# Stores issued from a loop, and x spread over block diagonals by masked ANDs, in a batched x yT product

## The chip, the cores and the metric

The kernel runs on one core of a Trainium2 chip. The metric is the device time of one execution in microseconds (us), smaller being better. Before the change it is 301.15 us, the median of three runs between 301.08 and 301.67 us.

## The reference

```python
batch, n_heads, seq_t, seq_s, channels = 8, 12, 512, 512, 64
# x, y: float32 [8, 12, 512, 64]
np.einsum('bhtc,bhsc->bhts', x, y).astype(np.float32)
```

There are 96 independent heads. For each of them a 512 x 64 matrix x is multiplied by the transpose of a 512 x 64 matrix y, which gives 512 x 512 float32 numbers. The inputs are 25.17 MB together and the output is 100.66 MB.

## The kernel before, in words

**Groups and halves.** The 96 heads are cut into NG = 6 groups of 16 heads. One load brings the x or the y of a group: 128 partitions with 16 KB each, 2 MB in all. So there are 12 loads, numbered n = 0 to 11, in the order x, y, x, y. Each group is computed in two halves, so there are NH = 12 steps i, and each step yields V = 4 output tiles of 2 MB (128 partitions x 4096 float32). That makes 48 stores, numbered o = 4*i + h.

**Buffers.** Five slots of 2 MB (`slots`) serve the loads first and the stores afterwards; results go into the four slots named in HOMES = (0, 2, 4, 1). ScalarE, VectorE and GpSimd cast the loaded float32 data to bf16 (`compress`): x goes to a tile `xk`, y is written in pairs into 32-bit words (`yb`). Two tiles `xb`, one for each half, hold x spread out for the product: every 32-bit word has two bf16 places, and in each 32-partition block only one of them is filled and the other stays zero from a memset at the start. `mix(i, name, part)` writes one of four 32-partition blocks of that spread with a strided copy on the engine `name`. VectorE then turns `xb` into `xT` and `yb` into `yT` in 32 x 32 blocks of 32-bit words (`transposes`).

**Products and evictions.** TensorE runs a loop of 6 turns (`products`), two steps in a turn, 32 matmuls a step, into two PSUM tiles `pm`. ScalarE runs a loop of 11 turns (`evictions`), one step in a turn: for each of the four output tiles it waits until the earlier store out of that slot has landed (semaphore `out`), then copies two PSUM tiles of 128 x 2048 float32 into the slot. The first step's evictions stand ahead of the loop, among the casts.

**Order.** The order of the work on each engine is the order in which the program emits it; `emit` derives the waits, and with `virtual=True` it only keeps the books for instructions that a loop issues. Up to load 11 the casts of all loads, the spreads of steps 0 to 2 (by GpSimd) and the first four results are interleaved by hand. After that `prepare(i)` puts on VectorE the two transposes of step i and the four spreads of step i + 1. SyncE issues every DMA: the 12 loads (`load`) and the 48 stores, one after another, each behind a wait on the semaphore `taken`, which counts evictions.

Of the kernel before, what the change touches and what calls it, by code (L numbers as in the profile page):

```python
# [10 lines left out]
def kernel(  # L11
# [22 lines left out]
    nc = tc.nc  # L34
    B, H, T, C = x.shape
    _, _, S, _ = y.shape
    P = 128
    G = 16
    Q = P // G
    R = T // Q  # L40
    NG = B * H // G
    NH = 2 * NG
    V = G // 4
    K = 8
    E = R // K
    D = 32
    SLOTS = 5
    HOMES = (0, 2, 4, 1)
    fp32 = mybir.dt.float32
    bf16 = mybir.dt.bfloat16  # L50
    u32 = mybir.dt.uint32
    COPY = mybir.ActivationFunctionType.Copy
    assert C == 2 * D and S == T and R == 2 * D and Q * V == D
# [3 lines left out]
    ov = out.rearrange("b h t s -> (b h t s)").rearrange(  # L57
        "(o u h q n) -> o h q u n", u=2, h=V, q=Q * E, n=K * S
    )

    sb = ctx.enter_context(tc.tile_pool(name="sb", bufs=1))
    ps = ctx.enter_context(tc.tile_pool(name="ps", bufs=1, space=bass.MemoryType.PSUM))
    slots = [sb.tile([P, K * S], fp32, name=f"slot{i}") for i in range(SLOTS)]
    xks = [sb.tile([P, R, C], bf16, name=f"xk{i}") for i in range(NG - 1)]
    ybs = [[sb.tile([P, R // 2 * D], u32, name=f"yb{h}{i}") for i in range(NG - 1 + h)] for h in range(2)]
    xbs = [sb.tile([P, K * E * D], u32, name=f"xb{half}") for half in range(2)]
    xTs = [sb.tile([P, K * D * E], u32, name=f"xT{i}") for i in range(2)]
    yTs = [sb.tile([P, D * R // 2], u32, name=f"yT{i}") for i in range(2)]
    pms = [ps.tile([P, 4, S], fp32, name=f"pm{i}") for i in range(2)]
    engines = {"act": nc.scalar, "dve": nc.vector, "pool": nc.gpsimd, "pe": nc.tensor, "sp": nc.sync}  # L70
# [3 lines left out]
    def sem(p):  # L74
        if p not in sems:
            sems[p] = tc.alloc_semaphore(p)
        return sems[p]
# [19 lines left out]
    def emit(name, make, reads=(), writes=(), dma=None, tells=None, virtual=False):  # L97

        points = [writer[r] for r in (*reads, *writes) if r in writer]
        points += [v for w in writes for v in readers.get(w, ())]  # L100
        if name == "pool" and name in ticks:
            points.append((name, ticks[name]))
        need(name, points, virtual)
        p, step = (tells or name, 1) if dma is None else (dma, 16)
        sem(p)
        at = (p, ticks.get(p, 0) + step)
        ticks[p] = at[1]
        snaps[at] = {**known[name], p: at[1]}
        if dma is None:
            own[name][p] = at[1]  # L110
            snaps[at].update(own[name])
        if not virtual:
            make().then_inc(sems[p], step)
        for r in reads:
            readers.setdefault(r, []).append(at)
        for w in writes:
            writer[w], readers[w] = at, []

    made_slots, loaded, asked = [], {}, []
    in_front = ["dve", "pool", "dve", "act"]  # L120

    def copy(name, dst, src, reads, writes, tells=None, virtual=False):
        emit(
            name,
            lambda: nc.scalar.activation(dst, src, COPY)  # L125
            if name == "act"
            else engines[name].tensor_copy(dst, src),  # L127
            reads,
            writes,
            tells=tells,  # L130
            virtual=virtual,
        )

    def both(i):
        return [("slot", i, 0), ("slot", i, 1)]
# [14 lines left out]
    def compress(n):  # L150

        i = loaded.pop(n)
        g = n // 2
        if n % 2 == 0:
            xk = g % (NG - 1)
            dst = xks[xk].rearrange("p r c -> p (r c)")
            copy("act", dst, slots[i], both(i), [("xk", xk)])
            return
        ys = slots[i].rearrange("p (r c) -> p r c", c=C)
        for half in range(2):  # L160
            b = g % (NG - 1 + half)
            yv2 = ybs[half][b].bitcast(bf16).rearrange("p (j c w) -> p j w c", j=R // 2, w=2)
            for ch in range(2):
                copy(
                    in_front[2 * half + ch],
                    yv2[ch * 64:(ch + 1) * 64],
                    ys[half * 64:(half + 1) * 64, :, ch * D:(ch + 1) * D].rearrange(
                        "p (j w) c -> p j w c", w=2
                    ),
                    both(i),  # L170
                    [("yb", half, b, ch)],
                )

    def mix(i, name, part):

        g, half = divmod(i, 2)
        ch, u = divmod(part, 2)
        lo = half * 64 + u * D
        xk = g % (NG - 1)
        xv2 = xbs[half].bitcast(bf16).rearrange("p (k e c u) -> p k e c u", k=K, e=E, u=2)  # L180
        copy(
            name,
            xv2[part * D:(part + 1) * D, :, :, :, u],
            xks[xk][lo:lo + D, :, ch * D:(ch + 1) * D].rearrange("p (e k) c -> p k e c", k=K),
            [("xk", xk)],
            [("xb", half, part)],
        )

    def transposes(i):
        g, half = divmod(i, 2)  # L190
        b = g % (NG - 1 + half)
        emit(
            "dve",
            lambda: nc.vector.transpose(  # L194
                xTs[half].rearrange("p (k r e) -> p k e r", k=K, e=E),
                xbs[half].rearrange("p (k e c) -> p k e c", k=K, e=E),
            ),
            [("xb", half, part) for part in range(4)],
            [("xT", half)],
        )  # L200
        emit(
            "dve",
            lambda: nc.vector.transpose(  # L203
                yTs[half].rearrange("p (r j) -> p j r", r=D),
                ybs[half][b].rearrange("p (j c) -> p j c", c=D),
            ),
            [("yb", half, b, ch) for ch in range(2)],
            [("yT", half)],
            tells="turned",
        )  # L210

# [20 lines left out]
    def rows(s, pm):  # L232
        return slots[s].rearrange("p (r s) -> p r s", s=S)[:, 4 * pm:4 * pm + 4, :]

    def evictions():

        act = mybir.EngineType.Activation
        with nc.Fori(0, NH - 1, engines=OrderedEngineSet([act])) as turn:  # L238
            filled, free = turn + 2, turn * 16 + 16
            for h, s in enumerate(HOMES):  # L240
                nc.scalar.wait_ge(sem(f"out{s}"), free)
# [4 lines left out]
    def result(o):  # L246

        i, h = divmod(o, V)
        s = HOMES[h]
        for pm in range(2):  # L250
            emit("pe", None, [("xT", i % 2), ("yT", i % 2)], [("pm", pm)], tells=f"pe{h}{pm}", virtual=True)
            want = {"turned": i + 1, "taken": 2 * o + pm + 1}
            assert all(want.get(p, 0) >= v for p, v in asked[-1].items()), (o, pm, asked[-1])
            copy("act", rows(s, pm), pms[pm], [("pm", pm)], [("slot", s, pm)], "taken", virtual=i > 0)
            want = {f"pe{h}{pm}": i + 1, f"out{s}": 16 * i}
            assert i == 0 or all(want.get(p, 0) >= v for p, v in asked[-1].items()), (o, pm, asked[-1])
        emit("sp", lambda: nc.sync.dma_start(ov[i, h], slots[s]), reads=both(s), dma=f"out{s}")

    def prepare(i):

        if i < NH:
            transposes(i)
        if i + 1 < NH:
            for part in range(4):
                mix(i + 1, "dve", part)

    with tc.tile_critical():  # L267
        sem("taken")
        ticks["taken"] = 2
        for g in range(SLOTS):  # L270
            load(g)
        for half, name in enumerate(("dve", "pool")):
            emit(
                name,
                lambda: engines[name].memset(xbs[half], 0.0),  # L275
                writes=[("xb", half, part) for part in range(4)],
            )
        for n in range(2 * NG):
            if n == 11:
                result(3)  # L280
            compress(n)
            mix(n // 4, "pool", n % 4)
            if n == 4:
                transposes(0)
            if n < 5:
                load(n + SLOTS)
            elif n in (6, 8):
                load(n // 2 + 7)
            elif n < 10:
                assert slot() == HOMES[n // 2 - 2]  # L290
            if n > 7 and n < 11:
                result(n - 8)
            if n == 9:
                transposes(1)
        prepare(2)
        for o in range(V, V * NH):
            result(o)
            if o % V == V - 1:
                prepare(o // V + 2)
        products()  # L300
        evictions()
        for name, i in zip(("dve", "pool", "sp", "act"), HOMES):
            need(name, [(f"out{i}", ticks[f"out{i}"])])


# [28 lines left out]
```

## Time and profile before

| What | us |
|---|---|
| median of 3 runs | 301.15 (301.08 to 301.67) |
| profiled execution | 301.3 |
| its span in the profile | 299.5 |
| busy: ScalarE | 212.2 |
| busy: VectorE | 151.9 |
| busy: TensorE matmuls | 143.5 |
| busy: GpSimd | 56.1 |
| DMA queue, share of the 16 DMA engines' span | 98.8% |

The span is the time between the first and the last recorded instruction; the profiled execution took 1.8 us more than its span. Busy times of the engines overlap. The DMA share is the time that packets took, over 16 engines times the span. A landing is the moment at which the semaphore of a DMA has received all its increments.

### The profile page before, as it was taken

The numbers are of one execution on the slowest core, as the hardware profiler recorded it, in microseconds if no ns is written. First come the engines' busy times: TensorE is split into PE (matmuls) and PEld (weight loads), VectorE is DVE, ScalarE is ACT, GpSimd is POOL, SyncE is SP. The second block draws the span as 40 slices with busy tenths as digits, with TensorE's granted clock in tenths as the row PEclk, the third lists the DMA queues.
The fourth block names the chain that finished last, engine by engine and source line by source line (L and its number), as shares of the span: only waits on it lengthen the run. The fifth ranks groups of instructions, "written<-read, shape, count | busy, mean of one in ns | idle before, by whom it ended". The sixth has DMA issues, their size and how long they took to land.

```text
span 299.5 us, 1309 instructions
## 1 busy us (share of the span) xinstructions
PE 143.5 (48%) x378; PEld 36.8 (12%) x384; DVE 151.9 (51%) x73; ACT 212.2 (71%) x109; POOL 56.1 (19%) x23
## 2 busy tenths in 40 slices
PE   0000040556666555667556566647576568576100
PEld 0000010111111111111111111111111111111000
DVE  2157897999839490760934908629159070000000
ACT  1665576999999868686867777776768686868500
POOL 2399999991000000000000000000000000000000
PEclk9999999978799786775686775685776855776855
DMA  7999999999999999999999999999999999999995
GB/s 274 429 429 433 429 429 425 429 429 427 431 435 427 429 438 427 429 433 431 429 435 431 423 433 435 427 427 438 427 422 433 429 425 429 431 424 425 429 427 217
DMA packets 8641, 125.84 MB, mean 420 GB/s; under 512 B 960, under 2 KB 960, under 8 KB 960
## 3 DMA queue, kind: packets, MB, share of 16 engines
q1 hardware_dynamic: 8640, 125.83, 98.8%
q14 instruction: 1, 0.01, 0.0%
HBM read 25.17 MB, written 100.66 MB: 420 GB/s over the span
## 4 chain that ended last, share of the span: by engine, by line
DMA 66%; ACT 17%; issue 7%; DVE 2%; PE 1%; SPq 0%; ACTq 0%
DMA out_dram<-slot 52%; ACT slot L244 12%; DMA slot<-in_y_dram 7%; DMA slot<-in_x_dram 6%; ACT slot L125 3%; DVE yb L127 2%; ACT yb L125 1%; PE pm L226 1%; ACT xk L125 1%; SPq L145 0%; ACTq L238 0%; ACTq L243 0%; ACTq L92 0%; SPq L329 0%; SPq L267 0%
## 5 line engine op out<-in xcount | busy, mean ns | idle before, releaser
L226 PE MATMUL pm<-yT,xT 128*128 128x512 bf16 x378 | 143.5, 524 | 135.2 <-ACT slot L244 77.3
L244 ACT ACTIVATE slot<-pm 128x2048 f32<-128x2048 f32 x88 | 160.1, 1878 | 47.7 <-DMA out_dram<-slot 47.6
L194 DVE STREAM_TRANSPOSE xT<-xb 128x2048 uint32<-128x2048 uint32 x12 | 46.8, 3897 | 74.7 <-PE pm L226 72.3
L226 PEld LDWEIGHTS pm<-yT,xT 128*128 128x128 bf16 x384 | 36.8, 117 | 241.3 <-ACT slot L244 137.4
L127 DVE COPY xb<-xk 32x2048 bf16<-32x2048 bf16 x36 | 46.9, 1303 | 1.0
L127 DVE CAST yb<-slot 64x2048 bf16<-64x2048 f32 x12 | 36.2, 3017 | 16.9 <-DMA slot<-in_y_dram 16.7
L127 POOL COPY xb<-xk 32x2048 bf16<-32x2048 bf16 x12 | 36.3, 3023 | 10.4 <-ACT xk L125 9.6
L125 ACT ACTIVATE xk<-slot 128x4096 bf16<-128x4096 f32 x6 | 21.7, 3617 | 16.3 <-DMA slot<-in_x_dram 16.3
L203 DVE STREAM_TRANSPOSE yT<-yb 128x1024 uint32<-128x1024 uint32 x12 | 23.1, 1923 | 0.0
L125 ACT ACTIVATE yb<-slot 64x2048 bf16<-64x2048 f32 x6 | 14.8, 2462 | 5.1 <-DMA slot<-in_y_dram 5.1
L127 POOL CAST yb<-slot 64x2048 bf16<-64x2048 f32 x6 | 17.8, 2970 | 1.3 <-DMA slot<-in_y_dram 0.8
L125 ACT ACTIVATE slot<-pm 128x2048 f32<-128x2048 f32 x8 | 14.5, 1869 | 0.2 <-PE pm L226 0.2
L275 DVE MEMSET xb<- 128x2048 uint32 x1 | 1.8, 1765 | 1.4 <-SPq L267 1.4
L125 ACT ACT_TABLE_LOAD x1 | 1.3, 1283 | 0.9 <-SPq L267 0.9
L275 POOL MEMSET xb<- 128x2048 uint32 x1 | 1.8, 1805 | 0.5 <-SPq L267 0.5
L318 POOL MEMSET const-float32-0.0<- 128x1 f32 x1 | 0.1, 98 | 0.2 <-issue 0.2
L318 POOL MEMSET const-float32-1.0<- 128x1 f32 x1 | 0.1, 98 | 0.0
L318 POOL MEMSET const-bfloat16-1.0<- 128x1 bf16 x1 | 0.1, 98 | 0.0
L318 POOL MEMSET const-uint8-127<- 128x1 uint8 x1 | 0.1, 98 | 0.0
## 6 DMA issues: line engine op xcount, KB each, us to landing
out_dram<-slot SPq DMA_DIRECT2D x48, 2048.0 KB, 16.0
slot<-in_x_dram SPq DMA_DIRECT2D x6, 2048.0 KB, 17.6
slot<-in_y_dram SPq DMA_DIRECT2D x6, 2048.0 KB, 20.8
```

Of the source, the lines that this page charges most:

```text
L125: lambda: nc.scalar.activation(dst, src, COPY)
L127: else engines[name].tensor_copy(dst, src),
L194: lambda: nc.vector.transpose(xTs[half].rearrange("p (k r e) -> p k e r", k=K, e=E), xbs[half].rearrange("p (k e c) -> p k e c", k=K, e=E),),
L203: lambda: nc.vector.transpose(yTs[half].rearrange("p (r j) -> p j r", r=D), ybs[half][b].rearrange("p (j c) -> p j c", c=D),),
L226: last = nc.tensor.matmul(pms[k // 4][:, j, :], xT[:, k + j, h, :], yT[:, h * S:(h + 1) * S], start=True, stop=True,)
L244: nc.scalar.activation(rows(s, pm), pms[pm], COPY).then_inc(sem("taken"), 1)
L275: lambda: engines[name].memset(xbs[half], 0.0),
L318: nc = _bacc.Bacc("TRN2", target_bir_lowering=False, num_devices=1)
```

## The change

Four things change together.

- **Stores.** The 44 stores of steps 1 to 11 are no longer written out on SyncE one by one. SyncE runs a loop of 11 turns whose body holds 4 waits and 4 stores, with the output address and the awaited count computed from the turn.
- **Spreads on VectorE.** For steps 4, 5, 7, 8, 10 and 11 the four strided copies are replaced by two `tensor_tensor` ANDs (`masked`). Each AND covers 64 partitions and 64 x 32 x 2 elements of 16 bits: x is read with every element twice, and a per-partition mask tile `keep` sets one of the two to zero.
- **Spreads on GpSimd.** For steps 3, 6 and 9 GpSimd makes the four strided copies that VectorE made. GpSimd also makes both memsets of `xb`, and three small ones for `keep`. The spread is now stored in the order of x, and the reordering by k moved into the transpose; `yT` is turned ahead of `xT`, and the semaphore `turned` follows `xT`.
- **Casts.** For the y loads 1 and 3 the cast of the second half's first 64 partitions moves from VectorE to ScalarE.

```diff
+    BY_POOL = (3, 6, 9)
+    keep = sb.tile([P, 1], u32, name="keep")
...
-                    in_front[2 * half + ch],
+                    "act" if n < 4 and half else in_front[2 * half + ch],
...
-            xv2[part * D:(part + 1) * D, :, :, :, u],
-            xks[xk][lo:lo + D, :, ch * D:(ch + 1) * D].rearrange("p (e k) c -> p k e c", k=K),
+            xv2[part * D:(part + 1) * D, :, :, u],
+            xks[xk][lo:lo + D, :, ch * D:(ch + 1) * D],
...
+    def masked(i):
+        g, half = divmod(i, 2)
+        xk = g % (NG - 1)
+        rows = slice(half * 64, half * 64 + 64)
+        for ch in range(2):
+            src = xks[xk][rows, :, ch * D:(ch + 1) * D].bitcast(u16)
+            dst = xbs[half][ch * 64:ch * 64 + 64].bitcast(u16).rearrange("p (r c u) -> p r c u", c=D, u=2)
+            emit(
+                "dve",
+                lambda: nc.vector.tensor_tensor(
+                    dst,
+                    src.unsqueeze(3).to_broadcast([64, R, D, 2]),
+                    keep[rows].bitcast(u16).unsqueeze(1).unsqueeze(1).to_broadcast([64, R, D, 2]),
+                    mybir.AluOpType.bitwise_and,
+                ),
+                [("xk", xk), "keep"],
+                [("xb", half, 2 * ch), ("xb", half, 2 * ch + 1)],
+            )
...
-                xTs[half].rearrange("p (k r e) -> p k e r", k=K, e=E),
-                xbs[half].rearrange("p (k e c) -> p k e c", k=K, e=E),
+                xTs[half].rearrange("p (k r e) -> p e k r", k=K, e=E),
+                xbs[half].rearrange("p (e k c) -> p e k c", k=K, e=E),
...
+    def stores():
+        sp = mybir.EngineType.SP
+        with nc.Fori(0, NH - 1, engines=OrderedEngineSet([sp])) as turn:
+            there = ov[bass.ds(turn + 1, 1)].rearrange("o h q u n -> (o h) q u n")
+            for h, s in enumerate(HOMES):
+                nc.sync.wait_ge(sem("taken"), turn * (2 * V) + (2 * V + 2 * h + 4))
+                nc.sync.dma_start(there[h], slots[s]).then_inc(sem(f"out{s}"), 16)
...
-            for part in range(4):
-                mix(i + 1, "dve", part)
+            if i + 1 in BY_POOL:
+                for part in range(4):
+                    mix(i + 1, "pool", part)
+            else:
+                masked(i + 1)
...
-        for half, name in enumerate(("dve", "pool")):
+        for half in range(2):
             emit(
-                name,
-                lambda: engines[name].memset(xbs[half], 0.0),
+                "pool",
+                lambda: nc.gpsimd.memset(xbs[half], 0.0),
                 writes=[("xb", half, part) for part in range(4)],
             )
+        for some, bits in ((slice(P), 0xFFFF), (slice(D, 2 * D), 0xFFFF << 16), (slice(3 * D, P), 0xFFFF << 16)):
+            emit("pool", lambda: nc.gpsimd.memset(keep[some], bits), writes=["keep"])
...
         evictions()
-        for name, i in zip(("dve", "pool", "sp", "act"), HOMES):
+        stores()
+        for name, i in zip(("pe", "pool", "sp", "act"), HOMES):
```

More of the change, by code (lines that the diff above doesn't have):

```diff
@@ L48 @@
     HOMES = (0, 2, 4, 1)
+    BY_POOL = (3, 6, 9)
     fp32 = mybir.dt.float32
     bf16 = mybir.dt.bfloat16
+    u16 = mybir.dt.uint16
     u32 = mybir.dt.uint32
@@ L179, in mix @@
         xk = g % (NG - 1)
-        xv2 = xbs[half].bitcast(bf16).rearrange("p (k e c u) -> p k e c u", k=K, e=E, u=2)
+        xv2 = xbs[half].bitcast(bf16).rearrange("p (r c u) -> p r c u", c=D, u=2)
         copy(
             name,
-            xv2[part * D:(part + 1) * D, :, :, :, u],
-            xks[xk][lo:lo + D, :, ch * D:(ch + 1) * D].rearrange("p (e k) c -> p k e c", k=K),
+            xv2[part * D:(part + 1) * D, :, :, u],
+            xks[xk][lo:lo + D, :, ch * D:(ch + 1) * D],
             [("xk", xk)],
@@ L191, in transposes @@
         b = g % (NG - 1 + half)
-        emit(
-            "dve",
-            lambda: nc.vector.transpose(
-                xTs[half].rearrange("p (k r e) -> p k e r", k=K, e=E),
-                xbs[half].rearrange("p (k e c) -> p k e c", k=K, e=E),
[L197 to L200, printed above, removed]
         emit(
@@ L208, in transposes @@
             [("yT", half)],
+        )
+        emit(
+            "dve",
+            lambda: nc.vector.transpose(
+                xTs[half].rearrange("p (k r e) -> p e k r", k=K, e=E),
+                xbs[half].rearrange("p (e k c) -> p e k c", k=K, e=E),
+            ),
+            [("xb", half, part) for part in range(4)],
+            [("xT", half)],
             tells="turned",
@@ L256, in result @@
             assert i == 0 or all(want.get(p, 0) >= v for p, v in asked[-1].items()), (o, pm, asked[-1])
-        emit("sp", lambda: nc.sync.dma_start(ov[i, h], slots[s]), reads=both(s), dma=f"out{s}")
+        emit(
+            "sp",
+            lambda: nc.sync.dma_start(ov[i, h], slots[s]),
+            reads=both(s),
+            dma=f"out{s}",
+            virtual=i > 0,
+        )
+        assert i == 0 or all(p == "taken" and v <= 2 * o + 4 for p, v in asked[-1].items()), (o, asked[-1])
+    def stores():
[5 more added lines that the diff above has]
+                nc.sync.dma_start(there[h], slots[s]).then_inc(sem(f"out{s}"), 16)
     def prepare(i):
```

## The prediction

> **What bounds the kernel now.** The profiled execution took 301.3 us: a span of 299.5 and 1.8 around it. The median of the runs, 301.15, lies 0.15 below; I sum against the profile and take off that 0.15 at the end. I read the slices first.
>
> ```profile
> DMA  7999999999999999999999999999999999999995
> q1 hardware_dynamic: 8640, 125.83, 98.8%
> ```
>
> From the second slice to the last but one the 16 DMA engines are full. No engine comes near that (ScalarE 71%, VectorE 51%). So only three things can move the time: the head ahead of the first packet, the rate of the packets, the tail behind the last. The windows give the tail (columns: busy time and count of PE, PEld, DVE, ACT, POOL, then clock, DMA share, GB/s):
>
> ```profile
> 295.00:296.00 1.00, 0.00 (x0) 0.00 (x0) 0.00 (x0) 0.00 (x0) 0.00 (x0) 0.50 0.73 311
> 296.00:297.00 1.00, 0.00 (x0) 0.00 (x0) 0.00 (x0) 0.00 (x0) 0.00 (x0) 0.50 0.08 33
> 297.00:298.00 1.00, 0.00 (x0) 0.00 (x0) 0.00 (x0) 0.00 (x0) 0.00 (x0) 0.50 0.04 16
> 298.00:299.50 1.50, 0.00 (x0) 0.00 (x0) 0.00 (x0) 0.00 (x0) 0.00 (x0) 0.50 0.00 0
> ```
>
> A share of 0.08 to 0.04 is one of 16 engines at work: for two us the others have finished and one has not. The landing records agree: the last store's fifteenth increment came 1.66 us ahead of its sixteenth. For stores 12 to 16 of the 60 DMAs (loads counted) that gap is 0.02 to 0.08; from DMA 17 it grows by some 0.07 a store. The span is then: 2.0 of head to the first packet, 60.5 until the last load lands at 62.5, 235.8 for 48 stores (4.91 each), and 1.2 from the last landing to the end; sum 299.5.
>
> Next, how far the issues run ahead of the packets. The chain of waits (start, us, what), in the steady part:
>
> ```profile
> 142.78 1.88 ACT slot L244
> 144.66 0.02 issue
> 144.68 15.99 DMA out_dram<-slot
> 160.66 0.02 issue
> 160.69 0.77 ACT slot L244
> ```
>
> A store lands 16.0 us after its issue starts while a store lands every 4.92, so some 10.5 us of packets (16.0 less 4.9 and the 0.54 of the issue) are still ahead of it when its issue is over. A delay shorter than this in PSUM eviction, products or spreads reaches no packet. The cover is thinnest at the turn from loads to stores. By issue and landing records: store 14 has 3.3 us ahead of it, store 16 (the first of step 1) 3.0, store 18 5.3, store 20 8.2, store 22 10.6.
>
> Last, who waits for VectorE, and what the operations cost (busy us, mean ns):
>
> ```profile
> DVE xT L194 <- PE pm L226: 72.3, 10, 9.7
> PE pm L226 <- DVE yT L203: 37.0, 1, 37.0
> ...
> L194 DVE STREAM_TRANSPOSE xT<-xb 128x2048 uint32<-128x2048 uint32 x12 | 46.8, 3897 | 74.7 <-PE pm L226 72.3
> L127 DVE COPY xb<-xk 32x2048 bf16<-32x2048 bf16 x36 | 46.9, 1303 | 1.0
> L127 POOL COPY xb<-xk 32x2048 bf16<-32x2048 bf16 x12 | 36.3, 3023 | 10.4 <-ACT xk L125 9.6
> L203 DVE STREAM_TRANSPOSE yT<-yb 128x1024 uint32<-128x1024 uint32 x12 | 23.1, 1923 | 0.0
> L125 ACT ACTIVATE yb<-slot 64x2048 bf16<-64x2048 f32 x6 | 14.8, 2462 | 5.1 <-DMA slot<-in_y_dram 5.1
> ```
>
> VectorE waits for the products ten times, 7 us each; they wait for it once, at the very start. Only these rows are needed to cost the change.
>
> **The change part by part.**
>
> *Stores from a loop.* Before, SyncE starts a store every 4.92 us and is occupied 0.54 by it. A loop adds register work and a branch. SyncE has no such row; ScalarE's loop, at its turn from 86.94 to 87.25 in the chain, shows 0.31 us of branch, register work and issue gaps. I take 0.3 us a turn, between 0 (hidden in the wait for `taken`) and 2.2 (0.54 more for each of four stores, as if each issue doubled). Behind it on SyncE stands only the next store. The turn starts where SyncE waits anyway: between stores 15 and 16 it is idle from 72.76 to 78.40, 5.6 us, which takes in the loop's entry. Without that cover the entry would cut into the 3.0 us at store 16; in steady state the 10.5 us take it. Path cost: 0.
>
> *What the shorter program removes.* The trace's DMA records have one instruction packet within the measured work, 8 KB at 166.3 us, 0.31 long. One engine's landing in the store that ended at 170.5 slipped 0.44 behind it. That engine was not the one that ends last: the store's sixteenth landing came at its usual 4.92. So removing it is worth 0, or at most 0.44 where it had hit the last engine. I take 0.
>
> *Masked ANDs.* Six steps lose four copies (5.2 us) and gain two ANDs of 4096 16-bit elements. No row has an AND. Lowest price by the copy, 1303/2048 = 0.64 ns an element: 2.6 us. Highest by the transposes, 3897/2048 = 1.90 ns: 7.8 us. Nearest is the VectorE memset of 2048 words in 1765 ns (0.86 ns), a plain write of one element after another: 3.5 us, which I take. Three steps of the new pattern (two with ANDs, one by GpSimd) cost VectorE 3 x 5.82 of transposes plus 4 x 3.5 = 31.5 us, at the high end 48.7, against 33.1 before. Three steps last 59.1. Nothing is late next: the transposes of a step begin as soon as the products of two steps earlier end, and are wanted 19.7 us later. If the cover were gone, an AND past (59.1 - 17.5)/4 = 10.4 us would add to the kernel.
>
> [...]
>
> *Spreads by GpSimd.* Step 3, 6 or 9 takes 4 x 3.02 = 12.1 us, at most 4 x 3.46 = 13.8. GpSimd is idle after 68.6. A spread may start once the transpose two steps earlier has read `xb` and is wanted 33 us later, when VectorE turns it. Even if VectorE's ANDs shut GpSimd out meanwhile (2 x 7.8), 29.4 fits. For step 3 the start is 68.6 and the need, before, 87.0: 82.4 fits. Cost 0.
>
> *Casts, memsets, order of transposes.* ScalarE's two more casts of 2.46 us fall into these gaps:
>
> ```profile
> 18.49 3.62 ACT L125 ACTIVATE xk<-slot 128x4096 bf16<-128x4096 f32 x1 [2.45 <-DMA slot<-in_x_dram]
> 28.27 3.62 ACT L125 ACTIVATE xk<-slot 128x4096 bf16<-128x4096 f32 x1 [2.46 <-DMA slot<-in_x_dram]
> ```
>
> They fill them to 0.05 us; the loads that those casts release had over 13 us of packets ahead of them. VectorE is 2 x 2.9 us freer. GpSimd's memsets (1.8 more, and three of some 0.1) end by 5 us, its first copy starts at 12.4. The transpose with other strides is priced as before: `yT`, with yet other strides, costs 1.88 ns an element and `xT` 1.90. The first step becomes ready up to 3 us earlier, but ScalarE evicts it only at 51.4, behind its own casts, so the first store stays at 55.0. ScalarE's work from 47.9 to 96.6, which sets the thin cover, is unchanged.
>
> Sum: 299.5 + 0 + 1.8 = 301.3 profiled, 301.15 as a median; I write 301.1.
>
> **The rivals.**
>
> *The uneven engine.* The last engine's lag starts as ScalarE's second loop turn begins (86.9) and stops growing near 250. For: I cannot name its cause, the issue path changes, and once the last issue is out (282.5) the lag shrinks from 1.80 to 1.66. Against: 0.07 a store is even, not tied to the one instruction packet, and issue, size and addresses stay. If it went, the tail's 1.66 would go: 299.5. If half went: 300.3. That is the faster case.
>
> *A fetch for each turn.* SyncE's branch back could make one DMA engine fetch the body again. By the one packet seen that is 0.44 us a turn on one engine, 11 turns: 4.8. It costs in full if it hits the last engine (306); on another it decides once it exceeds the 1.66 of lag, from the fourth turn on: 304.3. This is the slower case. For: SyncE never branched in its stores before. Against: the loops of TensorE and ScalarE make 17 turns and the trace has one packet.
> [...]
>
> *VectorE or GpSimd becomes the bound.* It needs an AND above 10.4 us. At 12 us three steps last 65.5 instead of 59.1; over three such groups, less the 10.5 us in hand, that adds some 9: 310. Against: no VectorE row, however slow per element, gives over 7.8.
>
> **How the numbers follow.** A difference below 0.2% (0.6 us) is about what a measurement of this kernel can tell from none. No measurable change: 0.52, 300.6 to 301.7 for the jitter of the runs and the 0.44 of a fetch on the wrong or right engine. Uneven engine eased, faster: 0.28. Fetch for each turn: 0.12, VectorE or GpSimd late: 0.08, both slower. The range runs from 299.4, the whole lag gone, to 302.0, two fetches on the last engine; it leaves out the slower cases' bulk, 0.2.
>
> **What would show it.** Right: DMA share 98 to 99%, 8640 packets of the queue as before, ANDs between 2.6 and 7.8 us, VectorE still waiting for products and not they for it, the first store at 55, stores landing 16 us after issue, and at most one instruction packet. Wrong: a slice below 9 in the DMA row after 60 us (the cover failed), instruction packets at every turn, more packets or smaller ones from the computed address, or a share of 0.04 to 0.08 in the last windows that is gone or twice as long.

## The result, and the profile after

The kernel after the change takes 302.22 us (median of 10 runs, 301.96 to 302.54). The kernel before, run beside it, takes 301.55 (301.08 to 301.76). The ratio is 1.0023, 95% interval 1.0013 to 1.0033: slower by 0.67 us. I had forecast 301.1, no measurable change, and a range that ended at 302.0.

The profiled execution took 302.1 us: a span of 299.8 and 2.3 around it, where before had 299.5 and 1.8. So of the 0.8 us between the two profiles 0.3 lie in the span and 0.5 outside. The runs list their spans, so this split can be made for many of them; "before" here is the 33 runs beside e1 to e4 below. "Around" is the time less the span:

| Kernel | span, mean | around, mean |
|---|---|---|
| before (33 runs) | 299.62 | 1.83 (1.73 to 1.97) |
| after (10 runs) | 299.82 | 2.38 (2.31 to 2.55) |

The span of one kernel varies from run to run by some 0.7 us (before 299.3 to 300.0); from that spread I estimate these means to be good to about 0.05 us.

The page's DMA lines after the change:

```profile
DMA  7999999999999999999999999999999999999995
...
q1 hardware_dynamic: 8640, 125.83, 98.7%
```

The queue is as full as before and moves the same 8640 packets: nothing ran dry. The windows at the end:

```profile
295.00:296.00 1.00, 0.00 (x0) 0.00 (x0) 0.00 (x0) 0.00 (x0) 0.00 (x0) 0.50 0.73 311
296.00:297.00 1.00, 0.00 (x0) 0.00 (x0) 0.00 (x0) 0.00 (x0) 0.00 (x0) 0.50 0.09 33
297.00:298.00 1.00, 0.00 (x0) 0.00 (x0) 0.00 (x0) 0.00 (x0) 0.00 (x0) 0.50 0.04 16
```

One DMA engine is again alone at the end, now for 1.83 us behind the fifteenth instead of 1.66. Single traces differ by more than that (e4 below, which has the stores of before, shows 2.05), so the cost is read from means over runs. Who waits for whom (us, times, longest):

```profile
DVE yT L217 <- PE pm L249: 62.4, 9, 14.4
...
PE pm L249 <- DVE xT L226: 33.6, 1, 33.6
```

The groups that are new or changed (busy us, mean ns, idle before):

```profile
L130 POOL COPY xb<-xk 32x2048 bf16<-32x2048 bf16 x24 | 80.4, 3352 | 77.8 <-DVE xT L226 69.0
...
L202 DVE TENSOR_TENSOR xb<-xk,keep 64x4096 uint16<-64x4096 uint16 x12 | 57.2, 4771 | 0.3
L217 DVE STREAM_TRANSPOSE yT<-yb 128x1024 uint32<-128x1024 uint32 x12 | 23.5, 1955 | 62.5 <-PE pm L249 62.4
L226 DVE STREAM_TRANSPOSE xT<-xb 128x2048 uint32<-128x2048 uint32 x12 | 46.5, 3874 | 3.0 <-POOL xb L130 3.0
```

VectorE waits for the products nine times (ten before), and they wait for it once, as before. An AND takes 4.8 us on average: ten of the twelve take 4.4, and two, each beside a copy on GpSimd, 6.5.

```profile
92.50 8.87 DVE L202 TENSOR_TENSOR xb<-xk,keep 64x4096 uint16<-64x4096 uint16 x2
...
L202 DVE TENSOR_TENSOR xb<-xk,keep x12: 4395/4421/6553, 92.5 to 230.7; 64x4096 uint16<-64x4096 uint16 x12
```

The new stores on SyncE (duration in ns, minimum, median, maximum, then first and last start):

```profile
L296 SPq FUSED_REGOPS  x44: 37/37/52, 78.5 to 282.8; - x44
L296 SPq MOVE out_dram<-slot x44: 29/29/29, 78.6 to 282.9; - x44
L296 SPq DMA_DIRECT2D out_dram<-slot x44: 546/547/570, 78.6 to 282.9; - x44
```

Two register instructions, the first of which also waits, stand before every store, and with the rest of the register work and the branch SyncE executes 4.5 instructions a store instead of 1. The first loop store starts at 78.6 instead of 78.4, and its cover is 2.8 us instead of 3.0. None of this delays a packet. The landing records do show a difference. Each DMA raises its semaphore by sixteen increments (960 landing records for 60 DMAs in before); I call them its landings, and the sixteenth the last landing. From DMA 19 to DMA 55 (counted from 0, the loads included) the last landings are 4.931 us apart on average, before 4.924.

### The profile page after: what moved, and what is told of

It is laid out like the page before. It is cut to its first block, busy times and chain, and to the rows that moved or that the text cites. A ratio compares the mean times of both kernels' runs of the same rounds, so it can differ in the third digit from the quotient of the medians.

```text
span 299.8 us, 1455 instructions
## 1 busy us (share of the span) xinstructions
PE 144.6 (48%) x384; PEld 36.9 (12%) x384; DVE 149.0 (50%) x46; ACT 217.0 (72%) x111; POOL 104.5 (35%) x39
## 3 DMA queue, kind: packets, MB, share of 16 engines
q1 hardware_dynamic: 8640, 125.83, 98.7%
## 4 chain that ended last, share of the span: by engine, by line
DMA 65%; ACT 19%; issue 8%; PE 1%; SPq 1%; ACTq 0%
DMA out_dram<-slot 52%; ACT slot L267 12%; DMA slot<-in_y_dram 7%; DMA slot<-in_x_dram 6%; ACT yb L128 3%; ACT slot L128 3%; PE pm L249 1%; ACT xk L128 1%; SPq L148 0%; ACTq L261 0%; SPq L296 0%; ACTq L266 0%; ACTq L95 0%; SPq L374 0%; SPq L95 0%
## 5 line engine op out<-in xcount | busy, mean ns | idle before, releaser
L130 POOL COPY xb<-xk 32x2048 bf16<-32x2048 bf16 x24 | 80.4, 3352 | 77.8 <-DVE xT L226 69.0
L202 DVE TENSOR_TENSOR xb<-xk,keep 64x4096 uint16<-64x4096 uint16 x12 | 57.2, 4771 | 0.3
L130 DVE CAST yb<-slot 64x2048 bf16<-64x2048 f32 x10 | 24.4, 2441 | 31.2 <-DMA slot<-in_y_dram 31.1
L128 ACT ACTIVATE yb<-slot 64x2048 bf16<-64x2048 f32 x8 | 19.7, 2462 | 5.1 <-DMA slot<-in_y_dram 5.0
L130 POOL CAST yb<-slot 64x2048 bf16<-64x2048 f32 x6 | 20.0, 3330 | 2.0 <-DMA slot<-in_y_dram 1.6
L317 POOL MEMSET xb<- 128x2048 uint32 x2 | 3.6, 1805 | 0.6 <-SPq L309 0.5
## 6 DMA issues: line engine op xcount, KB each, us to landing
out_dram<-slot SPq DMA_DIRECT2D x48, 2048.0 KB, 15.9
```

The source lines that it names most:

```text
L202: lambda: nc.vector.tensor_tensor(dst, src.unsqueeze(3).to_broadcast([64, R, D, 2]), keep[rows].bitcast(u16).unsqueeze(1).unsqueeze(1).to_ ...
L317: lambda: nc.gpsimd.memset(xbs[half], 0.0),
```

## The experiments

Each was run beside the kernel before. "Instr. a store" are the recorded instructions of all engines between the last landings of DMA 19 and 55, for one store (up to 7 of 384 matmuls are missing from a trace, at most 0.2 a store); this column and the last come from one trace each, the others from all runs.

| Run | median, us | ratio (95% interval) | span, mean | around, mean | instr. a store | last landings apart, ns |
|---|---|---|---|---|---|---|
| e1 loop alone | 301.65 | 1.0010 (1.0000 to 1.0019) | 299.93 | 1.77 | 28.0 | 4932 |
| e2 without the loop | 301.83 | 1.0013 (1.0004 to 1.0022) | 299.44 | 2.42 | 24.0 | 4923 |
| e3 VectorE waits last | 301.90 | 1.0014 (1.0005 to 1.0023) | 299.93 | 1.91 | 27.5 | 4931 |
| e4 before, TensorE waits last | 301.48 | 0.9998 (0.9989 to 1.0007) | 299.57 | 1.85 | 24.4 | 4924 |
| e5 after, 4 memsets more | 301.95 | 1.0018 (1.0009 to 1.0027) | 299.94 | 2.01 | 27.5 | 4925 |
| e6 before, GpSimd drains | 303.82 | 1.0080 (1.0066 to 1.0094) | 301.96 | 1.89 | 47.0 | 4978 |
| e7 loop, SyncE drains | 303.37 | 1.0071 (1.0057 to 1.0085) | 301.74 | 1.75 | 35.9 | 4951 |
| e8 fewer matmuls | 300.31 | 0.9968 (0.9957 to 0.9980) | 298.53 | 1.90 | 13.9 | 4899 |
| e9 after, 12 memsets more | 301.96 | 1.0013 (1.0004 to 1.0022) | 300.01 | 1.91 | 27.6 | 4930 |
| e10 no loop, 12 memsets | 301.44 | 1.0000 (0.9991 to 1.0009) | 299.56 | 1.91 | 24.2 | 4923 |
| e11 last store cut | 302.14 | 1.0022 (1.0013 to 1.0031) | 300.36 | 1.76 | 24.7 | 4924 |
| e12 loops written out | 301.15 | 0.9989 (0.9980 to 0.9998) | 299.32 | 1.83 | 21.6 | 4917 |
| before | | | 299.62 | 1.83 | 24.5 | 4924 |

### The loop and the rest, one at a time

e1 is the kernel before with the loop of stores alone:

```diff
-        emit("sp", lambda: nc.sync.dma_start(ov[i, h], slots[s]), reads=both(s), dma=f"out{s}")
+        emit("sp", ..., virtual=i > 0)   # and stores(), as in the change
```

> The kernel before with the stores of steps 1 to 11 issued from the loop, and nothing else of the change. Theory A (the loop of stores lengthens what lies around the span): about 302.0 to 302.2, with the time less the span at 2.3 us as after the change, where before shows 1.8; the span near 299.5 to 299.8. Theory B (the work moved between VectorE, GpSimd and ScalarE slows the packets): within 0.2 us of before, time less span 1.8. Theory C (the engine that makes the last wait on store slot 0): as before, 1.8.

e2 is the change with these lines taken back.

> The kernel after the change with the stores written out one by one again: the masked ANDs, GpSimd's spreads, ScalarE's casts and TensorE's last wait stay. Theory A: as before, 301.5, time less span 1.8. Theory B: 302.0 to 302.2, the excess in the span. Theory C: 302.0 to 302.2, the excess around the span.

e3 is the change with the old last waits, and e4 the kernel before with the new ones:

```diff
-        for name, i in zip(("pe", "pool", "sp", "act"), HOMES):
+        for name, i in zip(("dve", "pool", "sp", "act"), HOMES):   # e3; e4 the other way round
```

> The kernel after the change, but VectorE instead of TensorE makes the last wait on store slot 0, as before. Theory A and theory B: as after the change, 302.2, time less span 2.3. Theory C: back at 301.5 to 301.7, time less span 1.8.

> The kernel before, but TensorE instead of VectorE makes the last wait on store slot 0, as after the change. Theory A and theory B: as before, 301.5, time less span 1.8. Theory C: 302.0, time less span 2.3.

None of the three theories held as written; the span and what lies around it have to be told apart. The loop costs time in the span (e1: +0.31 over before; e3, which differs from e2 by the loop and the last wait: +0.49) and none around it (1.77). Theory A had it the other way. The rest of the change costs nothing in the span (e2: -0.18) but 0.59 around it (2.42). Theory B is refuted. The last wait alone does nothing (e4), yet in the changed kernel giving it back to VectorE takes the time around the span from 2.38 to 1.91 (e3). So there are two costs of some 0.3 to 0.5 us, and they come and go separately.

### The cost in the span: instructions slow one DMA engine

From DMA 19 to DMA 40 the first twelve landings of a store are 4.863 to 4.870 us apart from those of the next, whatever the kernel. The last landing takes 4.92 us in before and 4.93 after the change, and falls behind. (From DMA 43 to DMA 55 the first twelve slow down as well, to 4.91 us in before and in e6 alike; no run shows why. The late engine still ends last.) The loop adds 3.5 instructions a store and 8 ns. I tested whether instructions as such do this, on engines that have nothing to do with the stores (e6, e8) and on SyncE (e7).

e6 adds idle instructions on GpSimd:

```diff
+    with nc.Fori(0, NH - 1, engines=OrderedEngineSet([pool])) as turn:
+        for h in range(V):
+            nc.gpsimd.wait_ge(sem("taken"), turn * (2 * V) + (2 * V + 2 * h + 4))
+            nc.gpsimd.sem_inc(sem("spare"), 1)
+            for _ in range(20):
+                nc.gpsimd.drain()
```

> The kernel before with 20 drains, one semaphore increment and the loop's register work for each of the 44 later stores added on GpSimd, which is idle then; no data is touched. Theory D (the DMA engine that lands last loses some 2.2 ns for every instruction that any engine executes: 65 ns a store for about 25 instructions, 7 more for the 3.6 that the loop of stores adds): some 45 ns more a store, 4.92 becomes 4.965, the span grows by 2 us to 301.5, the time to 303.4. Theory E (the loss in the loop kernels comes from SyncE's own stores): as before, 301.45, 4.920 a store.

e7 adds them on SyncE:

```diff
                 nc.sync.dma_start(there[h], slots[s]).then_inc(sem(f"out{s}"), 16)
+                for _ in range(8):
+                    nc.sync.drain()
```

> The kernel before with the stores of steps 1 to 11 in the loop (as the loop alone) and eight drains on SyncE behind each store of the loop. Theory D: 8 more instructions a store, 18 ns: 4.927 becomes 4.945 a store, the time 301.7 becomes 302.4. Theory E in the form that the computed address makes a store dearer: as the loop alone, 301.7 and 4.927.

e8 takes instructions away on TensorE, by leaving out matmuls, so most of its output is not the product:

```diff
-                        for j in range(4):
+                        for j in range(4 if half == 0 and h == 0 else 1):
```

> The kernel before with three of four matmuls left out in all but the first output tile of every second step, so that most of the output is not the reference's; evictions, stores and all waits stay. Some 10 instructions a store fewer on TensorE. Theory D: 23 ns less a store, 4.92 becomes 4.90, the time 300.4 to 300.9. Theory E: as before, 301.45 and 4.920.

Theory D holds in all three, with a further cost in e7. First e6, the drains on GpSimd (duration in ns, minimum, median, maximum, first and last start):

```profile
L240 POOLq DRAIN  x880: 34/34/167, 78.4 to 286.2; - x176
```

And the windows at its end:

```profile
296.00:297.00 1.00, 0.00 (x0) 0.00 (x0) 0.00 (x0) 0.00 (x0) 0.00 (x0) 0.50 0.08 33
297.00:298.00 1.00, 0.00 (x0) 0.00 (x0) 0.00 (x0) 0.00 (x0) 0.00 (x0) 0.50 0.08 33
298.00:299.00 1.00, 0.00 (x0) 0.00 (x0) 0.00 (x0) 0.00 (x0) 0.00 (x0) 0.50 0.04 16
299.00:300.00 1.00, 0.00 (x0) 0.00 (x0) 0.00 (x0) 0.00 (x0) 0.00 (x0) 0.50 0.08 33
```

The drains move no data and nobody waits for them. Yet one DMA engine is now alone for 4.07 us, and the kernel is 2.4 us longer. In e8, whose trace has 811 instructions instead of 1309, it is alone for 0.60 us (windows):

```profile
295.00:296.00 1.00, 0.00 (x0) 0.00 (x0) 0.00 (x0) 0.00 (x0) 0.00 (x0) 0.50 0.66 279
296.00:297.00 1.00, 0.00 (x0) 0.00 (x0) 0.00 (x0) 0.00 (x0) 0.00 (x0) 0.50 0.04 16
```

A straight line through all the traces but that of e12 is 4.865 us + 2.39 ns for each instruction in a store's time. Its start is what the other engines take up to DMA 40, so the whole lag of the late engine is accounted for. The points at 13.9, 24.5, 35.9 and 47.0 instructions lie within 1.3 ns of the line; e5 is the farthest, 5 ns below, in a trace whose span is the shortest of its eleven runs. The mean spans, which take in every run, say the same: a line through them (without e7 and e11, whose ends differ) rises 0.104 us for each instruction a store, or 2.37 ns over 44 stores, and all lie within 0.10 us of it, e5 within 0.03.

e7 came 1.0 us above what theory D gives. Its landings show why: they are 4.951 us apart, as the line says (8 x 2.39 = 19 ns a store, 0.8 us in all), but the last store's last landing is 5.70 behind the one before it. An 8 KB instruction packet stands at 298.9 in that trace. All other engines are done by then, and it lies between the late engine's last data packet and the packet of 4 bytes that ends the store. This is the case that the prediction priced at 0.44 us; in this trace it was 0.8. The other four runs of e7 have no trace.

### The cost around the span: VectorE's last instruction fetch

The DMA records show packets of 8 KB of instructions. In before one comes at 166.3 us, when VectorE has executed 59 recorded instructions, and one 1.6 us behind the span's end. The records do not name the engine that fetches, and no run shows the late one to be SyncE's, as the expectation of e10 has it. But in all eight traces with VectorE's old casts and copies one comes behind VectorE's 59th instruction, whatever the other engines have executed by then; so I put it down to VectorE. In after and e2 it is not there, and one comes 2.2 us behind the span's end. In after VectorE has only 56 recorded instructions. So I lengthened its stream.

```diff
+        for k in range(4):        # e5; 12 in e9 and e10
+            emit("dve", lambda: nc.vector.memset(spare[:, k:k + 1], 0), writes=[("spare", k)])
```

> The kernel after the change with four more VectorE instructions, memsets of 128 x 1 words to a spare tile at the very start, where VectorE is idle. In the traces so far VectorE fetches 8 KB of instructions after its 59th recorded instruction; VectorE has 93 in the kernel before and 56 after the change, where the fetch comes 2.2 us after the span's end. Theory F (the place of that fetch in VectorE's stream): with 60 instructions the fetch moves into the span, the time less the span falls from 2.38 to about 1.8 and the kernel to about 301.65. Theory G (VectorE ends early because it no longer makes a last wait): nothing changes, 302.2 and 2.38.

> The kernel after the change with twelve tiny VectorE memsets at the start instead of the four of the run before. Theory F, corrected (VectorE's fetch of its next 8 KB of instructions ends the execution; 4 instructions moved it from 2.21 to 1.79 us behind the span's end, 0.1 us each): with 12 it lies 1 us or more ahead of that and is hidden by the waits of the end; the time less the span falls to the 1.75 of the kernels that show no fetch at the end, the time to 301.6 to 301.7. Theory G (VectorE ends early): the time less span stays at 2.0 or above.

> The change without the loop of stores, with the twelve VectorE memsets: both costs found so far are out. Theories D and F: span 299.45, time less span 1.8 to 1.85 (SyncE's own fetch, 1.6 us behind the end, stays), 301.25 to 301.3, or 0.05% below the kernel before: the masked ANDs, GpSimd's spreads and ScalarE's casts cost nothing by themselves. If one of these parts has a cost of its own, 301.5 or more.

| Run | VectorE, recorded | its fetch | around, us |
|---|---|---|---|
| e2 | 56 | 2.24 behind the end | 2.42 |
| after | 56 | 2.21 behind the end | 2.38 |
| e3 | 57 | none in the trace | 1.91 |
| e5 | 60 | 1.79 behind the end | 2.01 |
| e9 | 68 | at 146.9 | 1.91 |
| e10 | 68 | at 146.3 | 1.91 |

In e2, after and e5 the time around the span is 0.17 to 0.22 us more than the fetch's distance from the end. I had expected 4 memsets to move the fetch into the span; it moved 0.42 us forward, and only with 12 did it move in. That takes 2.38 - 1.91 = 0.47 us off the time around the span, with nothing changed but VectorE's stream, and theory G, by which memsets change nothing, is refuted: in e9 VectorE does not make the last wait either. My expectation of 1.75 was 0.16 too low, and with it the time of e9. e10 has neither cost and equals the kernel before (1.0000, interval 0.09% to either side): the ANDs, GpSimd's spreads and ScalarE's casts cost and bring nothing that shows.

What places the fetch is not shown. It comes behind VectorE's 59th recorded instruction in before, but behind the 45th in e9 and e10, and 60 instructions did not bring it into the span in e5, so theory F holds only in that the length of VectorE's stream matters. e3 has one instruction more than after, shows no fetch, and gains as much as twelve memsets; I have not settled why. Nor does every late fetch go with a longer time: e12 below has one 1.84 us behind the end, of an engine that I can't tell, and 1.83 us around. The remaining 0.06 us of e9 and e10 over the kernel before stay open too.

### Two attempts at a better kernel

e11 is meant to give the late engine less of the last store. That store becomes three: half of each row for all 128 partitions, then the other half for partitions 0 to 119, and that for 120 to 127.

```diff
...
+            for rows_, cols in ((P, slice(0, half)), (P - 8, slice(half, 2 * half)), (-8, slice(half, 2 * half))):
...
```

> The kernel before with the last store cut in three: half of each row for all 128 partitions, then the other half for partitions 0 to 119 and for 120 to 127 alone. If the packets of the last eight partitions are the ones that the late DMA engine carries, and the small piece goes to other engines, the late engine gets 4 half packets less: the tail of 1.66 us shrinks by about 1.0 to 1.2 us, 300.3 to 300.5. If the late engine is another one, the tail stays or grows by up to 0.6 us: 301.4 to 302.1.

It is slower, 0.04 us above what was expected at most if the late engine is another one. The trace doesn't decide that: of the 256 half packets, 0.31 us long as a rule, 49 took over 0.5, and the last landings came from the pieces themselves. Which engine is late stays open.

e12 writes out the loops of TensorE and ScalarE.

```diff
-        with nc.Fori(0, NH // 2, engines=OrderedEngineSet([pe])) as turn:
+        for turn in range(NH // 2):
...
-        with nc.Fori(0, NH - 1, engines=OrderedEngineSet([act])) as turn:
+        for turn in range(NH - 1):
```

> The kernel before with TensorE's and ScalarE's loops written out: the same products and evictions, but no register work, and most waits stand in the instruction that they hold. By the order of instructions that is about 21.7 instead of 24.5 a store. Theory D (2.4 ns for each instruction on the late DMA engine): 7 ns less a store, 4.917, the span 0.3 us shorter, 301.15 us, faster than both kernels. [...]

It met the expectation: 301.15 us, 0.9989 of before (interval 0.9980 to 0.9998), and less than either kernel took. From its page:

```profile
span 299.6 us, 1165 instructions
...
q8 instruction: 3, 0.05, 0.1%
q14 instruction: 2, 0.02, 0.0%
```

144 instructions fewer than before bring 0.26 us in the mean span (299.58 in the runs beside it); three larger instruction fetches, of 16 KB and 0.96 us each, cost nothing that shows. The line fitted to the other traces gives 4.865 + 21.6 x 2.39 ns = 4.917 us a store, and 4.917 was measured. So a loop, which makes the stream short, is the dearer form here, for the stores (e1) and for products and evictions together (e12).

## Why the prediction was wrong

**What bounds the kernel: right.** DMA share, packets, the full queue from 60 us on, the cover (10.4 us in the steady part, 2.8 at its thinnest), the first store at 55.1 and 15.9 us from issue to landing came as read from before.

**The loop: wrong step.** "Path cost: 0" counted SyncE's own 0.3 us a turn and hid it in its waits. That part held. But the late DMA engine is on the path whatever the cover, and the runs show that it pays for instructions of GpSimd, SyncE and TensorE alike. By the fitted line the change's 27.6 - 24.5 = 3.1 instructions more a store, over 44 stores, cost 3.1 x 2.39 ns x 44 = 0.33 us; the mean span rose by 0.20 in the changed kernel, by 0.31 in e1 (0.37 by the line) and by 0.45 from e10 to e9, which differ by the loop alone. I had the lag's size and growth in hand (0.07 us a store) and set it down as a cause that I could not name. Dividing it by the 24.5 instructions a store would have suggested some 2.9 ns each (2.39 by the fitted line), and with it the sign of the change: more instructions, more lag. Instead I gave that rival to the faster side.

**Around the span: wrong step.** The sum took the 1.8 us as fixed. They rose to 2.4, and lengthening VectorE's shorter stream by twelve memsets took 0.47 of that back, as the fetch behind the end moved into the span. How a late fetch lengthens the time, and what places it, stays open. I had treated instruction packets only where they could hit a data packet (0 to 0.44 us). In the changed kernel the one at 166.3 is gone, as foreseen; no run shows that alone to be worth anything.

**The rival of a fetch for each turn: refuted.** After the change, and in e1, no instruction packet repeats with the turns: the DMA records of after have one in the span, at 0.1 us and of 32 bytes, and none in the 11 turns.

**The ANDs: mis-sized, without effect.** I took 3.5 us between 2.6 and 7.8; most are 4.4 and the average is 4.8. The nearest row, a memset of 2048 words in 1.77 us, gave 0.86 ns an element; an AND of 4096 elements in 4.42 us takes 1.08. The AND reads two operands and the memset none; no run shows what of the difference this makes.

**GpSimd: mis-sized, without effect.** The bound of 13.8 us for four spreads held for step 3 (with the last spread of step 2, five copies in 14.6 us) and not for steps 6 and 9, which took 18.4 and 18.1:

```profile
107.13 18.42 POOL L130 COPY xb<-xk 32x2048 bf16<-32x2048 bf16 x4 [27.38 <-DVE xT L226]
```

Beside ANDs four copies took 6.5 to 6.7 us, and the four others of these steps 2.5; of the four ANDs beside them the first of each pair took 4.4 us and the second 6.5. So in these two steps both engines lost time. The prediction's allowance of 29.4 us, for ANDs that shut GpSimd out, covers it.

**ScalarE, transposes: right.** A transpose takes 3.87 and 1.96 us (3.90 and 1.92 before). ScalarE's x casts started 0.11 and 0.16 us later, not 0.05.

## What to carry to other kernels

Where one resource is full from start to end, split the time into span and surroundings, and the resource into its members: here one DMA engine of sixteen set the end, and its lag is the part of the span that the change was seen to move. Count executed instructions, not only busy time: waits, register work and branches of a loop cost nothing that shows on their engine and still 2.4 ns each in this kernel, as far as recorded runs can tell. And look at what a shorter stream does to the last instruction fetch.

## What was not expected of the hardware

In the store phase one DMA engine loses 2.39 ns for every instruction executed, on GpSimd, SyncE or TensorE, also for drains that touch no data; VectorE and ScalarE were not varied alone. A packet of 16384 bytes takes that engine 611 ns (its last one in before), so by estimate 2.39 ns are the time of 2.39 x 16384 / 611 = 64 bytes; no run shows that any such bytes are moved. Every run of the experiments lists its span and so was recorded, and no run can show whether the loss belongs to the execution or to its recording.
